# A decoder layer on one core: where the differences of a weight matrix are formed, and in which order two stages get their operands

## The chip, the cores and the metric

One core of a Trainium2 chip runs the kernel. The metric is the device time of one execution in microseconds, lower is better. The engines are TensorE (PE; its weight loads are PEld in the profile), VectorE (DVE), ScalarE (ACT), GpSimd (POOL) and SyncE (SP), whose queue issues all the transfers of this kernel, in order.

## The reference

One layer in float32 over 16 meta tokens and 1024 tokens of width 2048 (batch 1), followed by a final norm that drops the meta tokens:

```python
h = rmsnorm(x, gain)
q, k, v, g_attn, u, g_pool, m_attn, m_pool = split(h @ w_in)
o_attn = stick_breaking_attention(q, k, v) * silu(g_attn)     # 8 heads of 128
y_attn = o_attn @ w_attn_up                                   # (1024 -> 2048)
o_pool = (multiscale_pool(u) @ pool_w) * pool_scale * silu(g_pool)
y_pool = o_pool @ w_pool_up                                   # (1024 -> 2048)
merged = sigmoid(m_attn) * y_attn + sigmoid(m_pool) * y_pool
out = rmsnorm(x + merged @ w_out, final_gain)
```

## The kernel before, in words

Every matrix product is done in three matmuls: each operand is split into a high part (ACT copies it to a shorter float, L116) and a low part (the difference, L117, on DVE or POOL), and high times high, high times low and low times high are summed in one accumulator (`mm3`, L137 to L140; the last stage writes the three out in L1007 to L1009).

The large products, by `w_in` and by `w_out`, are cut in two by two blocks and done with seven block products instead of eight (Strassen's scheme in Winograd's form). This needs sums of blocks of both factors. For `w_out` these are four differences per block position: with b11, b12, b21, b22 its four blocks, T1 = b12 - b11 (form 2), b12 - b22 (form 1), b11 - (b12 - b22) (form 0) and b21 - (b11 - (b12 - b22)) (form 3). They don't depend on the tokens. `w_forms` (L183) forms them on POOL (L194), 256 columns at a time, from blocks loaded by SP (L190), and stores them to DRAM in `d_wf` (L195); the last stage loads them as weights. `w_forms` is a generator, and its steps are taken between the products of the attention stage: `between[0]` is called behind each of the three products of a pair of column blocks (`duo`). Form 2 is made from b12 and b11 loaded a second time, since the first copies are overwritten.

The stages in order of time: norm and transposes; the projections by `w_in`; the pooling branch; the attention stage (1174 to 1910 us), which for each of eight heads finishes the head's projections and lets the attention of the head (`attention`, L733) run step by step between matmuls of the next projections; the merges; the last stage.

In a step of attention, `scores` (L734) has PE form the scores, ACT two sigmoids (L743, L744), POOL mask the diagonal block (L748), DVE run a product scan (L753) and a product (L754), and two steps later `turn` (L763) has PE transpose the result (L769) for a split (L116, L117) and the product with the values.

The merges (1910 to 2275 us) do 32 products in the order of the list `order`: for a block of 128 output columns, `p` is the pooling branch (by `w_pu`) and `a` the attention branch (by `w_au`). Each has two halves of 512 tokens, 24 matmuls each, and two weight tiles that `load_w` loads and splits (`wr`, `wh`, `wl`, four buffers each). DVE multiplies each result by its gate (`sp`, `sa`, six buffers each, L965 and L970), POOL adds the two branches (L971), and for every second `a` product `sums` (L943) has POOL form four sums (L949) and SP store seven tensors to `d_f` (L957). The operands `op` and `oa` are filled ahead of the loop by `fill` (L908): a load to `ol` (six buffers) and a split.

The last stage multiplies by `w_out`: `prod` (L1000) loads a weight tile per step `j`, and `step` fills the next operand (`fill_f`, L1013, tiles `mr`, two buffers) and loads a row of `x`. Its first operand is A11, filled ahead of the first product (L1036) from `d_f[0]`.

The order of the instructions on each engine's queue is set by the framework's scheduler, by data, buffers and place in the program; `tc.keep_in_program_order` pins an instruction behind the one traced before it on its engine, and `tc.issue_after(ins)` puts what its block traces on the engine of `ins` behind `ins`. Tiles of a pool that is opened later take the memory of pools that were closed.

Of the kernel before, what the change touches and what calls it, by code (L numbers as in the profile page):

```python
# [9 lines left out]
F32 = mybir.dt.float32  # L10
# [5 lines left out]
P = 128  # L16
# [56 lines left out]
def trunk_kernel(  # L73
# [109 lines left out]
    def w_forms(pool):  # L183

        for p, j, i in ((p, j, i) for p in range(2) for j in range(KH) for i in range(2)):
            c = slice(i * 256, (i + 1) * 256)

            def block_of(tag, kh, nh):
                t = pool.tile([P, 256], F32, tag=tag, name=nm("cw"), bufs=1)
                tc.keep_in_program_order(nc.sync.dma_start(t, w_block(p, j, kh, nh)[:, c]))  # L190
                return t

            def minus(n, a, b):
                tc.keep_in_program_order(nc.gpsimd.tensor_tensor(out=a, in0=a, in1=b, op=ALU.subtract))  # L194
                tc.keep_in_program_order(nc.sync.dma_start(w_form(n)(p, j)[:, c], a))  # L195
                return a

            b12, b22 = block_of("cw0", 0, 1), block_of("cw1", 1, 1)
            b11, b21 = block_of("cw2", 0, 0), block_of("cw3", 1, 0)
            yield  # L200
            t2 = minus(0, b11, minus(1, b12, b22))
            minus(3, b21, t2)
            yield
            b12, b11 = block_of("cw1", 0, 1), block_of("cw0", 0, 0)
            yield
            minus(2, b12, b11)
# [22 lines left out]
    with ExitStack() as actx:  # L229
# [343 lines left out]
        def duo_steps(d, dst, post, dstm=None, step=None, again=False):  # L573
# [4 lines left out]
            def part(tag, src):  # L578
                t = ub.tile([P, HALF], F32, tag=tag, name=nm(tag), bufs=1)
                nc.sync.dma_start(t, src[d.n])  # L580
                return t
# [43 lines left out]
        between = [lambda: None]  # L625

        def duo(*args):
            for call in duo_steps(*args):
                call()
                between[0]()  # L630
# [10 lines left out]
        with ExitStack() as a0ctx:  # L641
# [24 lines left out]
            def silu_duo(*args):  # L666
                for call in silu_steps(*args):
                    call()
                    between[0]()
# [51 lines left out]
        with tc.tile_pool(name="a1", bufs=1, side="right", reuse_waits="tile") as a1:  # L721
# [127 lines left out]
            forms = w_forms(a1)  # L849
            between[0] = lambda: next(forms, None)  # L850
# [40 lines left out]
            for _ in forms:  # L891
                pass
# [13 lines left out]
    with tc.tile_pool(name="pm", bufs=2, side="right", reuse_waits="tile") as pm:  # L906

        def fill(A, j, src):  # L908
            raw = pm.tile([P, 512], F32, tag="ol", name=nm("ol"), bufs=6)
            nc.sync.dma_start(raw, src)  # L910
            put(A, j, raw)

        def fill_up(A, d_o, t):
            for j in range(KH):
                fill(A, j, d_o[j][:, t * HALF : (t + 1) * HALF])

        def up_mm(w, o, c):

            ops = [load_w(w_src(w, q, c * P)) for q in range(2)]
# [15 lines left out]
        for n, k in enumerate((("p", 0), ("p", KH), ("p", 1))):  # L935
            order.remove(k)
            order.insert(n, k)
        op, oa = [xquads(0, HALF, xo), xquads(1, HALF, xo)], [xquads(2, HALF), xquads(3, HALF, xc)]
        for t in range(2):
            fill_up(op[t], d_op, t)  # L940
        sps, ms = {}, {}

        def sums(j):  # L943
# [12 lines left out]
            for n, t in enumerate((a11, a12, r2, r3, r1, a22, r4)):  # L956
                nc.sync.dma_start(d_f[n][j], t)  # L957

        for n, (kind, c) in enumerate(order):
            if n in (0, 1):  # L960
                fill_up(oa[n], d_oa, n)
            if kind == "p":
                gs = [gate("sp", 6, d_sp, c, t) for t in range(2)]
                for t, a in up_mm(w_pu, op, c):
                    nc.vector.tensor_tensor(out=gs[t], in0=a, in1=gs[t], op=ALU.mult)  # L965
                sps[c] = gs
            else:
                gs = [gate("sa", 6, d_sa, c, t) for t in range(2)]
                for t, a in up_mm(w_au, oa, c):
                    nc.vector.tensor_tensor(out=gs[t], in0=a, in1=gs[t], op=ALU.mult)  # L970
                    nc.gpsimd.tensor_tensor(out=gs[t], in0=gs[t], in1=sps[c][t], op=ALU.add)  # L971
                ms[c] = gs
                if c >= KH:
                    sums(c - KH)

# [59 lines left out]
    A11, A12 = xquads(0, HALF, xo), xquads(1, HALF, xo)  # L1035
    for call in fills((A11, 0)):  # L1036
        call()
# [147 lines left out]
```

## Time and profile before

| | |
|---|---|
| median of three runs | 2612.1 us (2606.89 to 2615.9) |
| the profiled execution, its own time | 2615.75 us |
| its span, first to last instruction | 2614.0 us |
| mean granted clock of PE | 0.983 |
| PE busy | 2468.5 us, 94% of the span |
| POOL busy | 1034.6 us, 40% |
| DVE, ACT busy | 1253.8 us, 896.0 us |
| moved by DMA | 466 MB, 178 GB/s over the span |

Busy time is the time in which an engine executes; waits, register work and the issue of transfers don't count. The span leaves out 1.75 us of the execution's own time. PE is the busiest engine by far, and a wait of another engine matters only where PE waits for what that engine makes.

### The profile page before, as it was taken

The page shows a single profiled execution, that of the slowest core. Times are in us where ns is not written, and L with a number is a line of the kernel's source. Part 1 is how long each engine was busy: PE and PEld are TensorE (multiplying, and loading weights), DVE is VectorE, ACT ScalarE, POOL GpSimd, SP SyncE. Part 2 cuts the span into 40 slices and gives each one's busy share as a digit, 9 for nine tenths or more (in the row PEclk, how much of TensorE's full clock was granted, in tenths as well). Part 3 has the DMA queues.
Part 4 walks back from the last instruction along what each step waited for, and adds up shares of the span by engine and source line. Part 5 has one row for each costly group of instructions (what it writes and reads, how often), then busy time and mean ns, then how long its engine had stood idle before and what let it go on. Part 6 is the DMA issues. An engine that isn't in the chain of part 4 may idle for free. (4 is left out here: it accounts for less than half of the span.)

```text
span 2614.0 us, 36254 instructions
## 1 busy us (share of the span) xinstructions
PE 2468.5 (94%) x12680; PEld 2088.1 (80%) x12680; DVE 1253.8 (48%) x2089; ACT 896.0 (34%) x1845; POOL 1034.6 (40%) x962
## 2 busy tenths in 40 slices
PE   6898999999999999899999999999889999899998
PEld 5676778888888887887887888888768888677887
DVE  5432234543333344675575566557652222255456
ACT  6421122222222234224454454445441111044243
POOL 1665555554454534235445544554303222210212
PEclk8999999999999999999999999999989999999999
DMA  5566555665555557436556656554575444375544
GB/s 179 162 206 214 192 192 204 216 226 180 182 182 177 185 186 219 126 126 187 178 174 183 187 165 191 182 177 141 164 239 173 138 143 135 116 238 185 183 132 169
DMA packets 418168, 466.24 MB, mean 178 GB/s; under 512 B 35505, under 2 KB 278577, under 8 KB 416945
## 3 DMA queue, kind: packets, MB, share of 16 engines
q1 hardware_dynamic: 417984, 463.93, 55.8%
q8 instruction: 99, 1.62, 0.3%
q14 instruction: 85, 0.69, 0.1%
HBM read 321.50 MB, written 142.31 MB: 177 GB/s over the span
## 5 line engine op out<-in xcount | busy, mean ns | idle before, releaser
L138 PE MATMUL acc<-x,wh 128*128 128x512 f32 (+2 forms) x2736 | 980.2, 359 | 27.6 <-ACT wh L116 18.5
L140 PE MATMUL acc<-x,wl 128*128 128x512 f32 (+2 forms) x2736 | 971.1, 355 | 8.9 <-DVE wl L117 7.5
L139 PE MATMUL acc<-x,wh 128*128 128x512 f32 (+2 forms) x2736 | 968.8, 354 | 0.0
L138 PEld LDWEIGHTS acc<-x,wh 128*128 128x128 f32 x2736 | 520.1, 190 | 98.6 <-ACT wh L116 24.2
L140 PEld LDWEIGHTS acc<-x,wl 128*128 128x128 f32 x2736 | 518.6, 190 | 86.4 <-DVE wl L117 14.5
L139 PEld LDWEIGHTS acc<-x,wh 128*128 128x128 f32 x2736 | 519.3, 190 | 62.8
L116 ACT ACTIVATE wh<-wr 128x512 fp32r<-128x512 f32 x408 | 256.4, 630 | 580.6 <-PE accb L139 273.2
L117 DVE TENSOR_TENSOR wl<-wr,wh 128x512 fp32r<-128x512 f32 x288 | 217.2, 756 | 241.4 <-ACT wh L116 230.2
L117 DVE TENSOR_TENSOR wl<-r,wh 128x512 fp32r<-128x512 f32 x160 | 150.4, 944 | 339.3 <-ACT wh L116 315.2
L271 POOL TENSOR_TENSOR r<-raw,raw 128x512 f32<-128x512 f32 x80 | 111.7, 1396 | 378.8 <-DMA raw<-in_w_in_dram 357.0
L116 ACT ACTIVATE wh<-r 128x512 fp32r<-128x512 f32 x160 | 100.3, 632 | 469.7 <-POOL r L271 363.8
L117 POOL TENSOR_TENSOR wl<-wr,wh 128x512 fp32r<-128x512 f32 x120 | 171.8, 1431 | 224.0 <-ACT wh L116 170.6
L271 POOL TENSOR_TENSOR r<-r,raw 128x512 f32<-128x512 f32 x160 | 221.4, 1384 | 12.5 <-DMA raw<-in_w_in_dram 2.5
L138 PE MATMUL accb<-x,wh 128*128 128x512 f32 x512 | 200.5, 392 | 12.4 <-ACT x L116 12.4
L139 PE MATMUL accb<-x,wh 128*128 128x512 f32 x512 | 200.7, 392 | 0.0
L140 PE MATMUL accb<-x,wl 128*128 128x512 f32 x512 | 200.2, 391 | 0.0
L1007 PE MATMUL accb<-wh,x 128*128 128x512 f32 x416 | 163.8, 394 | 15.6 <-ACT x L116 13.3
L753 DVE TENSOR_TENSOR_SCAN wt<-wt 128x272 f32<-128x272 f32 (+5 forms) x128 | 109.8, 858 | 142.9 <-POOL wt L748 105.0
L194 POOL TENSOR_TENSOR cw<-cw,cw 128x256 f32<-128x256 f32 x128 | 106.1, 829 | 172.5 <-DMA cw<-in_w_out_dram 152.4
L1009 PE MATMUL accb<-wl,x 128*128 128x512 f32 x416 | 164.0, 394 | 2.5 <-DVE wl L117 2.3
L1008 PE MATMUL accb<-wh,x 128*128 128x512 f32 x416 | 163.3, 393 | 0.0
L971 POOL TENSOR_TENSOR sa<-sa,sp 128x512 f32<-128x512 f32 x32 | 47.2, 1475 | 275.4 <-DVE sa L970 265.9
(176 smaller groups left out, 3124.0 us busy)
## 6 DMA issues: line engine op xcount, KB each, us to landing
raw<-in_w_in_dram SPq DMA_DIRECT2D x96, 512.0 KB, 6.0
d_r<-r SPq DMA_DIRECT2D x160, 256.0 KB, 2.0
wr<-d_r SPq DMA_DIRECT2D x160, 256.0 KB, 3.3
raw<-in_w_in_dram SPq DMA_DIRECT2D x152, 256.0 KB, 5.3
cw<-in_w_out_dram SPq DMA_DIRECT2D x192, 128.0 KB, 3.2
wr<-in_w_in_dram SPq DMA_DIRECT2D x80, 256.0 KB, 3.0
d_wf<-cw SPq DMA_DIRECT2D x128, 128.0 KB, 2.0
wr<-d_wf SPq DMA_DIRECT2D x64, 256.0 KB, 2.8
```

Source lines behind the costliest of these rows:

```text
L116: nc.scalar.activation(hi, src, AF.Copy)
L117: (eng or nc.vector).tensor_tensor(out=lo, in0=src, in1=hi.bitcast(F32), op=ALU.subtract)
L138: nc.tensor.matmul(ps, wh, rh, start=first, stop=False, skip_group_check=skip)
L139: nc.tensor.matmul(ps, wh, rl, start=False, stop=False, skip_group_check=skip)
L140: nc.tensor.matmul(ps, wl, rh, start=False, stop=last, skip_group_check=skip)
L194: tc.keep_in_program_order(nc.gpsimd.tensor_tensor(out=a, in0=a, in1=b, op=ALU.subtract))
L271: nc.gpsimd.tensor_tensor(out=t, in0=a, in1=b, op=ALU.add)
L753: nc.vector.tensor_tensor_scan(out=rev, data0=rev, data1=rev, initial=wt[:, w : w + 1], op0=ALU.mult, op1=ALU.bypass)
L971: nc.gpsimd.tensor_tensor(out=gs[t], in0=gs[t], in1=sps[c][t], op=ALU.add)
L1007: nc.tensor.matmul(a, sh, wh, start=first and j == 0, stop=False, skip_group_check=not first)
L1008: nc.tensor.matmul(a, sl, wh, start=False, stop=False, skip_group_check=not first)
L1009: nc.tensor.matmul(a, sh, wl, start=False, stop=j == KH - 1, skip_group_check=not first)
```

## The change

The four forms are made during the merges, from tiles of 512 columns, so in 16 rounds instead of 32; each block is loaded once (form 2 gets a tile of its own, `cw4`). One or two steps of the generator are taken behind each of the 32 products: the loads of a round behind one product, its four subtracts and stores behind the next. In the attention stage the hook `between` goes. The tiles `up` and `nu` of a product pair get two buffers each (the pool's default).

At the start of the merges the two gate tiles of the first product are requested first, then the operands; the weights of the first product are issued behind the sixth operand load. In the merges the tensors 0, 1 and 5 of `d_f` are stored as soon as they are there, not with the sums. A11 is loaded and split in the merges, through their `ol` tiles, behind the last but one product.

```diff
     def w_forms(pool):
-        for p, j, i in ((p, j, i) for p in range(2) for j in range(KH) for i in range(2)):
-            c = slice(i * 256, (i + 1) * 256)
+        for p, j in ((p, j) for p in range(2) for j in range(KH)):
             def block_of(tag, kh, nh):
-                t = pool.tile([P, 256], F32, tag=tag, name=nm("cw"), bufs=1)
-                tc.keep_in_program_order(nc.sync.dma_start(t, w_block(p, j, kh, nh)[:, c]))
+                t = pool.tile([P, 512], F32, tag=tag, name=nm("cw"), bufs=1)
+                tc.keep_in_program_order(nc.sync.dma_start(t, w_block(p, j, kh, nh)))
                 return t
-            def minus(n, a, b):
-                tc.keep_in_program_order(nc.gpsimd.tensor_tensor(out=a, in0=a, in1=b, op=ALU.subtract))
-                tc.keep_in_program_order(nc.sync.dma_start(w_form(n)(p, j)[:, c], a))
-                return a
+            def minus(f, out, a, b):
+                tc.keep_in_program_order(nc.gpsimd.tensor_tensor(out=out, in0=a, in1=b, op=ALU.subtract))
+                tc.keep_in_program_order(nc.sync.dma_start(w_form(f)(p, j), out))
             b12, b22 = block_of("cw0", 0, 1), block_of("cw1", 1, 1)
             b11, b21 = block_of("cw2", 0, 0), block_of("cw3", 1, 0)
             yield
-            t2 = minus(0, b11, minus(1, b12, b22))
-            minus(3, b21, t2)
+            t1 = pool.tile([P, 512], F32, tag="cw4", name=nm("cw"), bufs=1)
+            minus(2, t1, b12, b11)
+            minus(1, b12, b12, b22)
             yield
-            b12, b11 = block_of("cw1", 0, 1), block_of("cw0", 0, 0)
+            minus(0, b11, b11, b12)
+            minus(3, b21, b21, b11)
             yield
-            minus(2, b12, b11)
...
-                t = ub.tile([P, HALF], F32, tag=tag, name=nm(tag), bufs=1)
+                t = ub.tile([P, HALF], F32, tag=tag, name=nm(tag))
                 nc.sync.dma_start(t, src[d.n])
...
-        between = [lambda: None]
         def duo(*args):
             for call in duo_steps(*args):
                 call()
-                between[0]()
...
-            forms = w_forms(a1)
-            between[0] = lambda: next(forms, None)
...
             gate_duo(gates.pop(0), None)
-            for _ in forms:
-                pass
...
         def fill(A, j, src):
             raw = pm.tile([P, 512], F32, tag="ol", name=nm("ol"), bufs=6)
-            nc.sync.dma_start(raw, src)
+            ins = nc.sync.dma_start(raw, src)
             put(A, j, raw)
+            return ins
         def fill_up(A, d_o, t):
-            for j in range(KH):
-                fill(A, j, d_o[j][:, t * HALF : (t + 1) * HALF])
-        def up_mm(w, o, c):
-            ops = [load_w(w_src(w, q, c * P)) for q in range(2)]
+            return [fill(A, j, d_o[j][:, t * HALF : (t + 1) * HALF]) for j in range(KH)][5]
+        def up_mm(w, o, c, behind):
+            with tc.issue_after(behind.ins) if behind is not None else nullcontext():
+                ops = [load_w(w_src(w, q, c * P)) for q in range(2)]
...
+        first = [gate("sp", 6, d_sp, 0, t) for t in range(2)]
         op, oa = [xquads(0, HALF, xo), xquads(1, HALF, xo)], [xquads(2, HALF), xquads(3, HALF, xc)]
-        for t in range(2):
-            fill_up(op[t], d_op, t)
+        behind = [fill_up(op[t], d_op, t) for t in range(2)][0]
...
-            for n, t in enumerate((a11, a12, r2, r3, r1, a22, r4)):
+            for n, t in ((2, r2), (3, r3), (4, r1), (6, r4)):
                 nc.sync.dma_start(d_f[n][j], t)
+        forms = w_forms(pm)
         for n, (kind, c) in enumerate(order):
...
             if kind == "p":
-                gs = [gate("sp", 6, d_sp, c, t) for t in range(2)]
-                for t, a in up_mm(w_pu, op, c):
+                gs = [gate("sp", 6, d_sp, c, t) for t in range(2)] if n else first
+                for t, a in up_mm(w_pu, op, c, None if n else behind):
...
                 ms[c] = gs
+                nc.sync.dma_start(d_f[c // KH][c % KH], gs[0])
                 if c >= KH:
+                    nc.sync.dma_start(d_f[5][c - KH], gs[1])
                     sums(c - KH)
+            for _ in range(2 if n % 2 else 1):
+                next(forms, None)
+            if (kind, c) == ("p", KC - 1):
+                for _ in forms:
+                    pass
+                A11 = xquads(0, HALF, xo)
+                for j in range(KH):
+                    fill(A11, j, d_f[0][j])
...
-    A11, A12 = xquads(0, HALF, xo), xquads(1, HALF, xo)
-    for call in fills((A11, 0)):
-        call()
+    A12 = xquads(1, HALF, xo)
     R2, R3 = xquads(2, HALF), xquads(3, HALF, xc)
```

## Rows read from the trace of the kernel before

**Rows 1.** The first part of the page: the busy time of each engine, its share of the span and its number of instructions.

```profile
PE 2468.5 (94%) x12680; PEld 2088.1 (80%) x12680; DVE 1253.8 (48%) x2089; ACT 896.0 (34%) x1845; POOL 1034.6 (40%) x962
```

**Rows 2.** The table of stretches, cut at the borders of the attention stage, the merges and the last stage. Columns: the stretch and its length; busy us and instructions of PE, PEld, DVE, ACT and POOL; the granted clock of PE; the share of DMA; GB/s.

```profile
1174.00:1910.00 736.00, 699.44 (x4091) 606.46 (x4090) 448.85 (x908) 354.01 (x838) 345.46 (x460) 1.00 0.57 176
1910.00:2275.00 365.00, 352.10 (x1537) 290.03 (x1536) 106.65 (x161) 60.71 (x98) 81.88 (x61) 0.98 0.49 156
2275.00:2614.00 339.00, 313.14 (x1440) 258.25 (x1440) 179.99 (x310) 129.43 (x257) 58.33 (x41) 0.97 0.56 182
```

**Rows 3.** The waits of PE, the first three rows in the attention stage, the fourth in the merges, the fifth in the last stage. Columns: us in total, times, the longest.

```profile
PE tr L769 <- DVE bt L754: 15.1, 8, 3.4
PE tr L769 <- DVE wt L751: 11.2, 9, 2.1
PE tr L769 <- DVE aT L117: 6.6, 12, 0.8
PE accb L138 <- ACT x L116: 12.4, 1, 12.4
PE accb L1007 <- ACT x L116: 13.3, 1, 13.3
```

**Rows 4.** From the listing of PE in order of time, in the attention stage: the first and the last wait on L754, one on L117 and one on L751. Columns: start, us, engine, line, operation, tile, count, and in brackets the idle time before and what ended it.

```profile
1213.11 0.33 PE L769 MATMUL tr<-ident,bt 128*128 128x128 f32 x1 [2.07 <-DVE bt L754]
1217.17 0.44 PE L769 MATMUL tr<-ident,bt 128*128 128x128 f32 x2 [0.62 <-DVE aT L117]
1241.06 0.55 PE L769 MATMUL tr<-ident,bt 128*128 128x128 f32 x3 [1.09 <-DVE wt L751]
...
1840.18 0.43 PE L769 MATMUL tr<-ident,bt 128*128 128x128 f32 x1 [3.40 <-DVE bt L754]
```

**Rows 5.** All engines in order of time around the last wait on L754, without the rows that don't bear on it.

```profile
1833.73 1.30 POOL L647 TENSOR_TENSOR gs<-zz,sg 128x512 f32<-128x512 f32 x1
1833.93 0.38 SPq L190 DMA_DIRECT2D cw<-in_w_out_dram  x1
...
1838.19 0.72 POOL L194 TENSOR_TENSOR cw<-cw,cw 128x256 f32<-128x256 f32 x1 [3.12 <-DMA cw<-in_w_out_dram]
1838.86 0.29 POOL L748 TENSOR_SCALAR_AFFINE_SELECT wt<-wt 128x128 f32<-128x128 f32 x1
...
1839.19 0.52 DVE L753 TENSOR_TENSOR_SCAN wt<-wt 128x144 f32<-128x144 f32 x1 [7.83 <-POOL wt L748]
```

**Rows 6.** In the attention stage: POOL's wait for the blocks of w_out, the group of its subtracts (us busy, mean ns), and from the listings in order of time a split on POOL with a product of DVE beside it, and a product of the same shape while POOL stood idle.

```profile
POOL cw L194 <- DMA cw<-in_w_out_dram: 145.3, 52, 8.0
L194 POOL TENSOR_TENSOR cw<-cw,cw 128x256 f32<-128x256 f32 x127 | 105.4, 830 | 165.5 <-DMA cw<-in_w_out_dram 145.3 <-issue 8.1 <-PE tr L769 7.0
...
1603.63 1.29 POOL L117 TENSOR_TENSOR wl<-wr,wh 128x512 fp32r<-128x512 f32 x1
1603.92 1.41 DVE L754 TENSOR_TENSOR bt<-bt,wt 128x384 f32<-128x384 f32 x1
...
1888.72 0.56 DVE L754 TENSOR_TENSOR bt<-bt,wt 128x384 f32<-128x384 f32 x1
```

**Rows 7.** Around the border of the attention stage and the merges, in order of time: the first weight load of the merges on SP, the last gate store, the last block loads of w_out, their subtract, the operand loads of the merges, and PE's first matmul.

```profile
1880.83 2.91 SPq L124 DMA_DIRECT2D wr<-in_w_pool_up_dram  x2
...
1911.94 0.43 SPq L844 DMA_DIRECT2D d_sp<-st  x1
1912.41 1.16 SPq L190 DMA_DIRECT2D cw<-in_w_out_dram  x2
...
1917.13 0.72 POOL L194 TENSOR_TENSOR cw<-cw,cw 128x256 f32<-128x256 f32 x1 [7.03 <-DMA cw<-in_w_out_dram]
1918.31 13.81 SPq L910 DMA_DIRECT2D ol<-d_op  x16
...
1922.49 0.80 PE L138 MATMUL accb<-x,wh 128*128 128x512 f32 x1 [12.40 <-ACT x L116]
```

**Rows 8.** The table of stretches (columns as in rows 2) behind each of the two gaps.

```profile
1922.50:1928.90 6.40, 6.40 (x14) 4.75 (x15) 4.77 (x8) 4.35 (x7) 0.00 (x0) 0.50 0.84 275
1929.30:1935.00 5.70, 5.70 (x26) 4.49 (x25) 4.35 (x8) 4.33 (x7) 0.00 (x0) 1.00 0.86 278
2287.80:2294.20 6.40, 6.40 (x14) 4.76 (x15) 3.01 (x5) 2.46 (x4) 0.00 (x0) 0.50 0.83 276
```

**Rows 9.** Around the border of the merges and the last stage, in order of time: POOL's last adds, the operand loads of the last stage, PE's first matmul, and the ninth weight load of the last stage.

```profile
2279.52 2.60 POOL L949 TENSOR_TENSOR r<-r,sa 128x512 f32<-128x512 f32 x2
...
2283.06 0.88 SPq L1015 DMA_DIRECT2D mr<-d_f  x2
...
2287.77 0.80 PE L1007 MATMUL accb<-wh,x 128*128 128x512 f32 x1 [13.26 <-ACT x L116]
...
2294.55 0.42 SPq L124 DMA_DIRECT2D wr<-in_w_out_dram  x1
```

**Rows 10.** In the merges: two groups of POOL's adds (us busy, mean ns, idle before), and SP's waits (us in total, times, the longest).

```profile
L971 POOL TENSOR_TENSOR sa<-sa,sp 128x512 f32<-128x512 f32 x31 | 45.6, 1470 | 271.2 <-DVE sa L970 261.8 <-DMA wr<-in_w_pool_up_dram 9.4
L949 POOL TENSOR_TENSOR r<-r,sa 128x512 f32<-128x512 f32 x14 | 18.1, 1293 | 0.5
...
SPq L957 <- POOL sa L971: 107.5, 22, 5.9
SPq L124 <- DVE wl L117: 86.3, 45, 7.6
```

More of the change, by code (lines that the diff above doesn't have):

```diff
@@ L1 @@
 import math
-from contextlib import ExitStack
+from contextlib import ExitStack, nullcontext
 import concourse.bass as bass
@@ L668, in silu_duo @@
                     call()
-                    between[0]()
             def sil_tiles():
@@ L968, in trunk_kernel @@
                 gs = [gate("sa", 6, d_sa, c, t) for t in range(2)]
-                for t, a in up_mm(w_au, oa, c):
+                for t, a in up_mm(w_au, oa, c, None):
                     nc.vector.tensor_tensor(out=gs[t], in0=a, in1=gs[t], op=ALU.mult)
```

## The prediction, made before the change was run

> **What bounds the kernel now.** I read the page first. In a span of 2614.0 us TensorE (PE) is busy for 2468.5 us, 94% [rows 1]: what can be won without fewer matmuls is the idle time of PE, at most 146 us, and whatever its clock loses. Next the table of stretches [rows 2], cut at the stage borders: the attention stage (1174 to 1910 us) has PE busy for 699.4 of 736 us, the merges (1910 to 2275) for 352.1 of 365, the last stage for 313.1 of 339. So idle time near the change is 36.6, 12.9 and 25.9 us. Then the waits of PE in each of these stretches [rows 3]. In attention they are many and short, nearly all on one line, the transposes L769: 15.1 us on the product L754, 11.2 us behind the copy L751, 6.6 us behind the split L117. In the merges there is one wait, 12.4 us, the first matmul on the split of its operand; in the last stage again one large one, 13.3 us, of the same kind. Around both gaps the table of stretches shows the granted clock [rows 8]: 0.50 for the 6.4 us behind each gap (the 1.2 GHz level), 1.00 before and after.
>
> Now what each wait ends on. Attention has eight heads, and the listing of PE shows for each head the same three waits: eight of 0.9 to 3.4 us on L754, seven of 0.6 us on L117, eight of 0.7 to 2.1 us mostly on L751 (the first and the last, or one, of each kind in [rows 4]). The instructions of all engines around the last of the first kind [rows 5] show its cause: GpSimd (POOL) ends the gating product L647 at 1835.0 us, then stands in front of a subtract of w_out (L194) whose block was issued only at 1833.9 us and lands 3.1 us of idle time later; behind it in POOL's queue waits the mask L748, and behind that the scan L753, the product L754 and the transpose. I looked at the other fifteen waits of the first and third kind in the same view: in each, L748 runs directly behind an L194 that had waited 2 to 5 us. The sums agree: L194 waited 145.3 us for its blocks in this stage and took 105.4 us itself [rows 6].
>
> At the first border [rows 7] the queue of SP decides. The last gate store is issued at 1911.9 us; then come two block loads of w_out, and the store of their difference, which waits for the subtract at 1917.1 us. Only at 1918.3 us does the first operand load of the merges go out, and PE starts 4.2 us later. At the second border [rows 9] the operand loads of the last stage go out at 2283.1 us, behind the stores of the last sums (POOL's last add starts at 2279.5 us), and PE starts at 2287.8 us.
>
> **The change, part by part.** *The block work leaves the attention stage.* Removed are 128 subtracts, 192 loads and 128 stores of 128 KB. All eight waits of the first kind end on a mask held up by L194. In [rows 4, 5] the mask could start at 1835.1 us in place of 1838.9, so the transpose, 1.3 us behind it, would be ready at about 1836.4, and PE came for it at 1836.8 (1840.18 less its wait of 3.40). I count the whole 15.1 us. For the eight of the third kind the scan behind them gets 0.65 to 2.1 us earlier; of 11.2 us in that row (which holds a few others) I count 8. The 6.6 us behind L117 I do not count. Against this I set 3 us for waits that appear when PE arrives earlier (the next in line are L751 and the split of the transposed block). Together 20 us; bounds: 10 (only half of the first kind and a third of the third goes) and 29 (all three rows but the last four microseconds).
>
> On this term a rule of the Trainium skill bears. [Rows 6] show the product L754 at 1.41 us for 384 columns while POOL ran a split beside it and at 0.56 us for the same shape while POOL was idle. The Trainium skill, GPSIMD Engine Reference, section 1. Specifications, has POOL and VectorE (DVE) share their SBUF interfaces, with contention for DVE instructions that have two SBUF inputs; the rows agree. By that rule 105 us less of POOL work would also shorten DVE's part and take some 4 us of the waits behind L117; the sum below would be 41 us instead of 37.
>
> *The up and nu tiles of each product pair get a second buffer.* No wait of PE ends on them; 0.
>
> *The first border.* Without block loads at the end, the next thing behind the last gate store (1911.9) is, by the new order, two gate loads and six operand loads, 0.43 us each, then the weights of the first product, pinned behind the sixth operand. In the old run nothing of a later pool was issued before the last store of the stage before, while weights, which need no new pool, ran ahead from 1880.8 us on [rows 7], so I take the operand loads to stay behind that store. First operand: issued at about 1912.8 instead of 1918.3, so 5.5 us earlier. But now weights of the first product come after it: ten loads of 256 KB at the 275 GB/s of [rows 8] last 9.5 us, so that product could start near 1922 us, as now. The second product's weights are not pinned; if PE takes that one first, the start is at 1917 us, and the operand splits, which now share their queue with two more weights, hold it for about 2 us. I take 3.5 us; bounds 0 and 15 (the whole gap of 12.4 us and 3 us of low clock, 14 matmuls at 0.43 instead of 0.23 us apart, if the loads run ahead of the last store after all).
>
> *The second border.* The operands of the last stage (A11) are loaded through buffers of the merges, at the last but one product; their data were stored long before (the last of them one product earlier), and the tiles they fill come free in the middle of that product, some 16 us before PE ends the merges (32 products in the 352 us of [rows 2] are 11 us each, and one and a half of them are left). Eight loads and eight splits (0.63 us on ScalarE, 0.69 on DVE) fit in 16 us. So the gap of 13.3 us goes, with the low clock behind it: 3 us. What is late next: weights of the last stage. The ninth is issued at 2294.6 us [rows 9], behind loads that wait for buffers; with PE starting at 2274.4 it is needed 21.8 us later, at 2296.2, and is ready at about 2299. With eight operand loads fewer in that queue it should be earlier; I set 2 us against the gain. 14.4 us; bounds 8 (weights late three times) and 16.4.
>
> *The block work enters the merges.* 64 subtracts of 512 columns (1.29 us each by the adds L949 of [rows 10], 83 us), 64 loads and 64 stores of 256 KB. POOL is busy for 81.9 of 365 us there [rows 2]; with 83 us more it is at 45%. DMA: 156 GB/s become about 255, below the 275 of [rows 8]. Loads are traced one product ahead of their subtracts, 11 us against the 3 to 5 us they take, so POOL should not stand and wait as it did. SP's stores wait for POOL: four stores in 5.2 us at the end of every second product, 13 us when two adds L971 and four of the sums come first. Behind them wait weights and gates. The weights have four buffers, two products (21.8 us) of lead; the wait of the weight loads in [rows 10] is for a free buffer, not for data. Cost: 1 us; bounds 0 and 12.
>
> Sum: 20 + 3.5 + 14.4 - 1 = 37 us. The profiled execution took 2615.75 us, which gives 2578.8; the median of the runs before is 2612.1, 3.65 us lower, and from it the sum gives 2575. I forecast 2576 us.
>
> **Rivals.** (a) *The attention waits stay*: another load or the next instruction of DVE takes L194's place. For it: seven waits of 0.6 us end on DVE as it is. Against: in [rows 5] POOL has nothing else to do for 3.1 us. Gain 17 us, 2595 us. (b) *The second gap stays*: A11's loads keep their place in SP's queue behind the last sums' stores. For it: stores of the blocks are pinned there too. Against: their buffers are free. Gain 23 us, 2589 us. (c) *Both gaps close and attention loses all its waits*: 15 + 16.4 + 29 less 1, so 59 us, 2553 us; it needs operand loads ahead of the last gate store, against which [rows 7] speak. (d) *The merges starve*: SP stands in front of a block store while weights wait behind it, and PE, which has no cover there but the two products' lead, stops in each product. It decides from 1.2 us per product on (32 products, 37 us); at 2 us each the time would be 2639 us. For it: POOL work in that stage doubles and every store of it is pinned in SP's order. Against: no wait of PE in the merges now, and 107 us of SP's waits on POOL already pass unnoticed there.
>
> **How the numbers follow.** Forecast (2562 to 2590) 0.60; (a) 0.15; (b) 0.08; (c) 0.10; (d) 0.07. The range for 8 in 10 takes in the forecast's bounds, (b), (a) and part of (c): 2560 to 2597 us. A measurement of this kernel tells about 0.3%, 8 us, from no change. Faster by more than that: all but (d) and the edge of (a), 0.92; within it 0.04; slower 0.04, from (d).
>
> **What will show it.** Right: PE's waits on L769 fall from 33 us to below 15; the first matmul of the merges waits 6 to 12 us; the first one of the last stage waits under 2 us, at clock 1.00; no wait of PE between the borders. Wrong: waits on weight splits (wh, wl) in the merges or early in the last stage, a granted clock of 0.50 inside the merges, or POOL waiting for cw loads there.

## The result, and the profile after

The changed kernel takes 2591.6 us, median of 6 runs (2586.9 to 2597.7), beside 2613.3 for the kernel before on the same chips: a ratio of 0.9918, 95% interval 0.9897 to 0.9938, or 22 us less. Forecast were 2576 us in a range of 2560 to 2597. The range holds the time, but the sum behind it does not fit term by term: one term was too small by 10 us and one had the wrong sign. That the time lies in the range is in part luck: had attention given only the 20 us counted for it, and all else come as it did, the time would have been about 2602 us.

The profiled execution took 2589.8 us, its span 2588.1. First the same reading as [rows 1, 2], of the changed kernel: busy time of TensorE (PE) and POOL by the page, then the stretches, here cut exactly at PE's own borders: attention from its first transposes to its last product, the first gap, the merges, the last stage, and the low clock inside the last stage.

```profile
PE 2462.5 (95%) x12680; PEld 2087.6 (81%) x12680; DVE 1268.1 (49%) x2089; ACT 896.8 (35%) x1845; POOL 1005.4 (39%) x898
```

```profile
1182.10:1876.40 694.30, 683.82 (x3994) 596.13 (x3992) 443.71 (x893) 346.86 (x827) 227.17 (x329) 1.00 0.39 120
1876.40:1907.60 31.20, 0.07 (x2) 0.04 (x1) 16.69 (x26) 16.20 (x26) 0.00 (x0) 0.57 0.85 267
1907.60:2259.40 351.80, 350.48 (x1537) 289.62 (x1538) 111.42 (x146) 51.26 (x83) 167.49 (x123) 0.99 0.73 239
2259.40:2588.10 328.70, 313.09 (x1441) 256.91 (x1439) 176.29 (x302) 126.55 (x250) 59.63 (x43) 0.98 0.56 184
2292.70:2298.20 5.50, 5.50 (x14) 3.83 (x14) 2.94 (x5) 1.90 (x3) 0.00 (x0) 0.59 0.63 226
```

The attention stage of the kernel before, cut in the same way:

```profile
1185.80:1910.10 724.30, 687.73 (x3994) 594.66 (x3992) 443.19 (x896) 350.45 (x831) 337.88 (x453) 1.00 0.57 175
```

So attention is 30.0 us shorter. The gap in front of the merges grew from 12.4 us [rows 7] to 31.2. The gap in front of the last stage, 13.3 us [rows 9], is gone: PE ends the merges and goes on at once, at a clock of 1.00. The last stage itself became 2.5 us longer. From the start of attention on this is 1428.2 us before and 1406.0 after, 22.2 less; the stages ahead of attention, which the change does not touch, differ by 3.7 us between the two executions.

PE's waits after the change, to be held against [rows 3] (L764 was L769, L746 was L751, L1010 was L1007): columns are us in total, times, the longest.

```profile
PE accb L138 <- ACT wh L116: 32.4, 2, 31.1
PE accb L1010 <- ACT wh L116: 7.0, 3, 5.6
PE tr L764 <- DVE wt L746: 7.0, 9, 1.6
PE tr L764 <- DVE aT L117: 1.0, 2, 0.6
```

The waits on the product in attention (15.1 us) have no row left. Both large rows now end on `wh`, the split of a weight, where [rows 3] ended on `x`, an operand. SP's queue shows why, for the first of them, in order of time (start, us, engine, line, operation):

```profile
1872.42 5.75 SPq L839 DMA_DIRECT2D d_sp<-st  x2
1878.26 0.88 SPq L923 DMA_DIRECT2D sp<-d_sp  x2
1879.23 14.19 SPq L901 DMA_DIRECT2D ol<-d_op  x16
1894.01 6.69 SPq L901 DMA_DIRECT2D ol<-d_oa  x8
1900.75 0.97 SPq L124 DMA_DIRECT2D wr<-in_w_pool_up_dram  x2
...
1906.88 0.63 ACT L116 ACTIVATE wh<-wr 128x512 fp32r<-128x512 f32 x1 [0.21 <-DMA wr<-in_w_pool_up_dram]
...
1907.56 0.80 PE L138 MATMUL accb<-x,wh 128*128 128x512 f32 x1 [31.13 <-ACT wh L116]
```

The operand loads go out right behind the last gate store and two gate loads, as forecast. But the two weights of the first product, in [rows 7] on their way 31 us ahead of the last gate store, now stand behind 24 operand loads and go out 22.5 us behind that store.

### The profile page after: what moved, and what is told of

It reads as the page before. It is cut to its first block, busy times and chain, and to the rows that moved or that the text cites. A ratio compares the mean times of both kernels' runs of the same rounds, so it can differ in the third digit from the quotient of the medians.

```text
span 2588.1 us, 35874 instructions
## 1 busy us (share of the span) xinstructions
PE 2462.5 (95%) x12680; PEld 2087.6 (81%) x12680; DVE 1268.1 (49%) x2089; ACT 896.8 (35%) x1845; POOL 1005.4 (39%) x898
## 4 chain that ended last, share of the span: by engine, by line
PE 77%; DMA 7%; DVE 6%; POOL 3%; ACT 2%; issue 2%; SPq 0%; DVEq 0%; POOLq 0%; ACTq 0%
PE acc L138 17%; PE acc L140 17%; PE acc L139 17%; PE accb L138 4%; PE accb L139 4%; PE accb L140 4%; POOL r L270 3%; PE accb L1012 2%; PE accb L1011 2%; PE accb L1010 2%; DMA mr<-d_f 2%; DMA raw<-in_w_in_dram 2%; PE tr L764 1%; DVE s L692 1%; DVE x L117 1%
## 5 line engine op out<-in xcount | busy, mean ns | idle before, releaser
L140 PEld LDWEIGHTS acc<-x,wl 128*128 128x128 f32 x2736 | 518.3, 189 | 85.3 <-DVE wl L117 13.3
L117 DVE TENSOR_TENSOR wl<-wr,wh 128x512 fp32r<-128x512 f32 x288 | 221.1, 770 | 248.2 <-ACT wh L116 230.0
L117 DVE TENSOR_TENSOR wl<-r,wh 128x512 fp32r<-128x512 f32 x160 | 149.5, 938 | 345.6 <-ACT wh L116 328.5
L117 POOL TENSOR_TENSOR wl<-wr,wh 128x512 fp32r<-128x512 f32 x120 | 166.6, 1388 | 346.0 <-ACT wh L116 289.3
L1010 PE MATMUL accb<-wh,x 128*128 128x512 f32 x416 | 163.8, 394 | 7.1 <-ACT wh L116 7.0
L117 DVE TENSOR_TENSOR wl<-raw,wh 128x512 fp32r<-128x512 f32 x136 | 102.6, 765 | 100.9 <-ACT wh L116 100.8
L116 ACT ACTIVATE wh<-raw 128x512 fp32r<-128x512 f32 x160 | 97.6, 624 | 135.2 <-PE acc L139 100.3
```

Source lines behind the costliest of these rows:

```text
L116: nc.scalar.activation(hi, src, AF.Copy)
L117: (eng or nc.vector).tensor_tensor(out=lo, in0=src, in1=hi.bitcast(F32), op=ALU.subtract)
L140: nc.tensor.matmul(ps, wl, rh, start=False, stop=last, skip_group_check=skip)
L1010: nc.tensor.matmul(a, sh, wh, start=first and j == 0, stop=False, skip_group_check=not first)
```

## The experiments

The stages of each kernel are in one table, each row from one profiled execution: PE's own borders in us, and the sum from the start of attention on. The last column is the ratio of the median time to that of the kernel before on the same chips, with its 95% interval. The kernels ran on different chips, so a difference of two medians is given beside the difference of the sums where the two part.

| kernel | attention | first gap | merges | second gap | last stage | sum | ratio |
|---|---|---|---|---|---|---|---|
| before | 724.3 | 12.4 | 352.0 | 13.3 | 326.2 | 1428.2 | 1 |
| changed | 694.3 | 31.2 | 351.8 | 0 | 328.7 | 1406.0 | 0.9918 (0.9897 to 0.9938) |
| no_pin | 694.3 | 10.3 | 352.2 | 0 | 325.9 | 1382.7 | 0.9832 (0.9816 to 0.9848) |
| blocks_only | 694.3 | 8.8 | 356.8 | 13.2 | 326.6 | 1399.7 | 0.9896 (0.9879 to 0.9912) |
| borders_only | 725.8 | 34.2 | 350.0 | 0 | 325.8 | 1435.8 | 1.0042 (1.0022 to 1.0063) |
| late_a11 | 694.3 | 29.4 | 357.3 | 13.2 | 325.7 | 1419.9 | 0.9961 (0.9947 to 0.9975) |
| no_blocks | 694.3 | 31.1 | 350.1 | 0 | 325.5 | 1401.0 | 0.9876 (0.9860 to 0.9891) |
| no_pin_rows | 694.3 | 9.6 | 352.3 | 0 | 324.5 | 1380.7 | 0.9798 (0.9776 to 0.9820) |
| no_pin_spread | 694.4 | 10.5 | 352.5 | 0 | 323.2 | 1380.6 | 0.9792 (0.9771 to 0.9814) |

**The pin alone (no_pin).**

```
-                for t, a in up_mm(w_pu, op, c, None if n else behind):
+                for t, a in up_mm(w_pu, op, c, None):
```

> The changed kernel with one edit: the weights of the first product of the merges are no longer pinned behind the sixth operand load. Theory A (SP's order makes the first gap): with the pin the two weight loads stand behind 24 operand loads in SP's queue (issued at 1900.75 us, 22.5 us behind the last gate store), without it they run ahead of the last gate store as in the kernel before; PE then waits for the first operand alone, about 8 us in place of 31.1, and the operands behind it, 0.89 us apart, keep just ahead of it; about 21 us less than the changed kernel, 2570 us. Theory B (the operand loads set the start whatever the order): weights that run ahead only shift the operand loads, PE starts early and stops at every operand, and the first product ends where it ends now; less than 8 us gained, 2584 us or more.

Measured: 2569.0 us, 23 us less than the changed kernel; the interval of its ratio (0.9816 to 0.9848) lies clear of that of the changed kernel. SP's queue and PE's first matmul of the merges:

```profile
1867.62 0.37 SPq L124 DMA_DIRECT2D wr<-in_w_pool_up_dram  x1
...
1879.94 3.20 SPq L124 DMA_DIRECT2D wr<-in_w_attn_up_dram  x2
1883.23 0.46 SPq L839 DMA_DIRECT2D d_sp<-st  x1
1883.74 0.96 SPq L923 DMA_DIRECT2D sp<-d_sp  x2
...
1891.67 0.79 PE L138 MATMUL accb<-x,wh 128*128 128x512 f32 x1 [10.26 <-ACT x L116]
```

Eight weight loads, those of four products, again run ahead of the last gate store (1883.23 us; the rows show three of the eight), and the wait ends on an operand. PE does not stop at every operand behind it: the merges last 352.2 us, as before. Theory A holds. Of the 31.2 us, 20.9 were the place of the weights in the queue; the other 10.3 are the wait for the first operand, which goes out behind the last gate store.

**The block work alone (blocks_only).** The kernel before, with `w_forms` in its new form and these edits to the two stages:

```
...
-            forms = w_forms(a1)
-            between[0] = lambda: next(forms, None)
...
+        forms = w_forms(pm)
...
+            for _ in range(2 if n % 2 else 1):
+                next(forms, None)
...
```

> The kernel before with one part of the change alone: the block work of w_out leaves the attention stage and stands in the merges, in its new form; the gate loads, the pin, the sums' stores and the loads of the last stage stay as before. Theory A (the gain in attention comes from the block work alone): the waits of PE on the transposes fall from 33 us to about 8 as in the changed kernel and attention ends some 33 us earlier; the weights of the first product, not pinned, run ahead, so the first gap is 8 to 9 us in place of 12.4; the second gap stays at 13 us with 3 us of low clock: about 36 us less than before, 2577 us, so faster than the changed kernel by some 15 us. Theory B (the block work starves the merges unless the rest of the change stands beside it, or the second buffers of up and nu have a share in attention): waits of PE between the borders or transposes still waiting over 15 us, 2595 us or more.

Measured: 2584.1 us, 29 us less than before, and attention at 694.3 us, although up and nu have one buffer here: their second buffer is worth nothing. The first gap is 8.8 us, as theory A said. The merges are 5 us longer than before, by one late weight 50 us into them (3.5 us) and the low clock behind it; on that point theory B is right in kind. By the traces this one part of the change gives more than the whole change, 28.5 us in place of 22.2; the intervals of the two ratios overlap.

**The rest of the change alone (borders_only).** The changed kernel with the block work put back into attention, in its old form, and with one buffer each for `up` and `nu`:

```
...
+            forms = w_forms(a1)
+            between[0] = lambda: next(forms, None)
...
-        forms = w_forms(pm)
...
```

> The changed kernel with one part undone: the block work stands in the attention stage as in the kernel before (up and nu with one buffer again); the gates ahead of the operands, the pin, the sums' stores and the early loads of A11 stay. Theory A (the parts add up): attention takes 724.3 us as before; at the first border the last block loads and their store still hold the operand loads back as they did (12.4 us), and the pin puts the weights behind 24 operand loads, 21 us more; at the second border 10.6 us are won as in the changed kernel. 12 us more than before, 2624 us. Theory B (the block work in attention and the pin hide behind one another: while SP waits for the last blocks the weights would not have been late): the first gap stays near 15 us, 2605 us, a little less than before.

Measured: 2624.5 us, 10 us more than before. The first gap is 34.2 us, and it ends on a weight again:

```profile
1914.12 0.33 SPq L195 DMA_DIRECT2D d_wf<-cw  x1
1914.54 0.88 SPq L932 DMA_DIRECT2D sp<-d_sp  x2
1915.47 14.77 SPq L910 DMA_DIRECT2D ol<-d_op  x16
1930.57 6.23 SPq L910 DMA_DIRECT2D ol<-d_oa  x8
1936.85 0.99 SPq L124 DMA_DIRECT2D wr<-in_w_pool_up_dram  x2
```

Theory A holds: the last store of the blocks holds the operand loads until 1915.5 us, 7 us behind PE's end (1908.3), and then the weights come as late behind them as in the changed kernel. The parts add up: -28.5 us (blocks_only) and +7.6 us give -20.9, against -22.2 for the whole.

**What in the block work cost attention 30 us.** Three kernels made from the one before, read in the attention stage alone, one execution of each. All three leave out the differences of `w_out`, so what they return is not the layer's result. The first keeps subtracts and stores, and loads blocks once; each subtract takes the fourth block from itself (att_noload):

```
...
-            b12, b22 = block_of("cw0", 0, 1), block_of("cw1", 1, 1)
-            b11, b21 = block_of("cw2", 0, 0), block_of("cw3", 1, 0)
...
+            if b is None:
+                b = block_of("cw0", 0, 1), block_of("cw1", 1, 1), block_of("cw2", 0, 0), block_of("cw3", 1, 0)
...
```

> The kernel before with all subtracts and stores of the block work left in the attention stage, but only four block loads in all, at its start (each later subtract takes the fourth of these blocks from itself, so the differences of w_out are left out). POOL's work stays, its wait for blocks goes. The attention stage, from its first transposes to its last product, takes 724.3 us before and 694.3 us with the block work moved away. Theory A (the waits come from a subtract that stands and waits for its block): nearly the whole gain is there, 694 to 698 us, with no wait on L754 left. Theory B (POOL's 105 us of subtracts, by standing ahead of the masks or by slowing DVE, make up a good part of the 30 us): 704 to 715 us, with waits on L754 and behind the splits L117 still there.

The second keeps loads and stores without a subtract (att_nosub):

```
-                tc.keep_in_program_order(nc.gpsimd.tensor_tensor(out=a, in0=a, in1=b, op=ALU.subtract))
```

> The kernel before with all block loads and stores left in the attention stage and no subtract (the loaded block itself is stored, so the differences of w_out are left out). Nothing of the block work is left on POOL; the DMA traffic and SP's queue stay as they are. Theory A (POOL's queue is the cause, for whichever reason): the attention stage takes 694 to 697 us in place of 724.3. Theory C (the traffic of 176 GB/s, or SP standing in front of block stores, makes weights and other loads late): 705 us or more, with POOL free of waits for blocks.

Measured: 700.1 us, between the two theories, and 694.7 us, as theory A said. So the traffic and SP's queue cost 0.4 us, and it is POOL. But the first run did not take all waiting away: its subtracts waited for the store of the tile they write.

```profile
POOL cw L195 <- DMA d_wf<-cw: 72.3, 24, 5.1
```

So the third keeps the subtracts alone: two blocks are loaded once, every subtract takes one from the other, and nothing is stored (att_subonly):

```
...
-                tc.keep_in_program_order(nc.sync.dma_start(w_form(n)(p, j)[:, c], a))
...
```

> The kernel before with the 128 subtracts of the block work alone left in the attention stage: two blocks are loaded once, nothing is stored, and every subtract takes one of them from the other (the differences of w_out are left out, the last stage takes a block of w_out itself in their place). No subtract waits for a load or for a store. The attention stage takes 724.3 us before, 694.3 with the block work moved away, 700.1 with subtracts and stores alone, where POOL still stood 72 us in front of tiles whose store had not landed. Theory A (waiting is all of it): 694 to 696 us. Theory B (POOL's time in subtracts, standing ahead of the masks, makes the rest): 698 to 701 us, with the waits behind the copy and the splits as in the run with the stores.

Measured: 703.4 us. PE's waits in attention, and POOL's subtracts:

```profile
PE tr L764 <- DVE wt L746: 12.8, 9, 1.6
PE tr L764 <- DVE aT L117: 1.9, 4, 0.7
...
L189 POOL TENSOR_TENSOR cw<-cw,cw 128x256 f32<-128x256 f32 x125 | 103.0, 837 | 0.6
```

No subtract waits (0.6 us idle ahead of 125 of them), no wait on the product is left, and still 9.1 of the 30.0 us remain, more than the 4 to 7 of theory B. So it is theory B in kind: 20.9 us went with the loads, the stores and the waits for them, and as loads and stores without a subtract cost 0.4 us, these were subtracts that stood waiting; 9.1 us are left with POOL's 103 us of work itself. The split is not sharp: the first run, where POOL waited 72.3 us for stores, was 3.3 us shorter than this one, so something beside waiting and working time counts, perhaps when a subtract runs. No run shows what. Of the 9.1 us, 5.8 stand in the row on L746 (12.8 us, 7.0 in the changed kernel). Whether POOL's work costs by standing ahead of the masks or by slowing DVE (below) the runs do not separate.

**A11 as before (late_a11).**

```
-                A11 = xquads(0, HALF, xo)
-                for j in range(KH):
-                    fill(A11, j, d_f[0][j])
...
+    for call in fills((A11, 0)):
+        call()
...
```

> The changed kernel with one part undone: the operands A11 of the last stage are loaded as before, behind the stores of the last sums. Theory A (the early loads take the whole second gap away, and a late weight gives back part): PE waits about 13 us for the first operand of the last stage, with 3 us of low clock behind it, and the wait of 5.6 us on a weight at 2292 us with its 2.3 us of low clock goes; about 9 us more than the changed kernel, 2600 us. Theory B (the second gap only moved into the late weight): within 3 us of the changed kernel, 2589 to 2595 us.

Measured: 2603.7 us, 12 us more than the changed kernel (13.9 by the sums). The second gap is back at 13.2 us and the last stage is 3.0 us shorter. Theory A holds. The merges are also 5.5 us longer: the second product waits 3.1 us for its weight, where it waits 1.3 us in the changed kernel, and behind that wait PE runs for 6.6 us at a clock of 0.54, where the changed kernel keeps 1.00 behind its shorter one (first the wait, then the stretch behind it):

```profile
1927.43 0.79 PE L138 MATMUL accb<-x,wh 128*128 128x512 f32 x1 [3.05 <-ACT wh L116]
1927.40:1934.00 6.60, 6.57 (x17) 5.20 (x18) 1.89 (x3) 1.64 (x3) 0.00 (x0) 0.54 1.07 362
```

That is 1.7 us of wait and 3.7 us of PE's busy time. The first gap is 1.8 us shorter here, so PE comes sooner for a weight that goes out as late behind that of the first product (16.0 us, 15.3 in the changed kernel). Why the first weights land sooner the edit does not explain, and it stays open.

**No block work at all (no_blocks).**

```
-        return lambda p, j: d_wf[n][p][:, j * 512 : (j + 1) * 512]
+        return lambda p, j: w_block(p, j, 0, 0)
...
-        forms = w_forms(pm)
+        forms = iter(())
```

The differences are left out, and the last stage loads a block of `w_out` in the place of each.

> The changed kernel without any block work: no loads, subtracts or stores of blocks of w_out, and the last stage takes a block of w_out itself wherever it took a difference (so that part of the computation is left out; the products and weight loads of the last stage stay as many). Theory A (in the merges the block work costs nothing, and the late weight of the last stage comes from SP's order there): the first gap 31 us less 2 for the four block loads between, the late weight as it is; within 4 us of the changed kernel, 2587 to 2592 us. Theory B (its traffic, 242 GB/s where there were 156, makes operands and weights late): the wait of 5.6 us with its 2.3 us of low clock goes, and 2 to 4 us more, 2580 us or less.

Measured: 2580.1 us. By the traces 5 us are won, 1.7 in the merges and 3.2 in the last stage; by the medians 12. Neither theory gives this: the median is about theory B's, but the wait on the late weight of the last stage, which theory B takes away, is still there without any block traffic:

```profile
2288.03 0.50 PE L1010 MATMUL accb<-wh,x 128*128 128x512 f32 x1 [4.60 <-ACT wh L116]
```

So the block work is not its cause; that it is the order of the queue (theory A) is tried next. But the block work is not free: 5 us by the traces, 12 by the medians.

**The late weight of the last stage (no_pin_rows, no_pin_spread).** In the changed kernel SP's queue runs so, at the start of the last stage:

```profile
2268.85 1.35 SPq L124 DMA_DIRECT2D wr<-in_w_out_dram  x3
2270.24 0.43 SPq L1018 DMA_DIRECT2D mr<-d_f  x1
...
2286.31 0.33 SPq L1018 DMA_DIRECT2D mr<-d_f  x1
2286.68 0.43 SPq L984 DMA_DIRECT2D row<-in_x_dram  x1
2287.15 0.43 SPq L124 DMA_DIRECT2D wr<-in_w_out_dram  x1
...
2292.68 0.79 PE L1010 MATMUL accb<-wh,x 128*128 128x512 f32 x1 [5.63 <-ACT wh L116]
```

Ten weights have gone out by 2270.2 us; the eleventh (the expectations call it the ninth, its number in the kernel before) stands behind seven operand loads, which go out as one of two buffers comes free, and the ten row loads between them. SP's largest wait from the start of the last stage to 2300 us is that of the operand loads for the split that frees a buffer:

```profile
SPq L1018 <- DVE x L117: 11.5, 8, 2.4
```

Two edits, each to the kernel without the pin: row loads eight steps later, and operands and rows both spread over twice the steps.

```
-[lambda b=b, c=c: load_row(0, b, c) for c in range(4) for b in range(HB)]
+[lambda: None] * 8 + [lambda b=b, c=c: load_row(0, b, c) for c in range(4) for b in range(HB)]
```

> The changed kernel without the pin, and in the last stage the sixteen loads of rows of x (256 KB each) begin eight steps later. Theory A (the ninth weight is late because in SP's queue it stands behind eight operand loads and eight row loads, which at 0.95 us each last 15 us): with the eight row loads out of the way it goes out some 7 us earlier, the wait of 5.1 us and its low clock go: 7 us less than without the pin alone, 2562 us. Theory B (the pace of the queue there is that of the operand loads alone, which wait for their two buffers, 2.2 us each): the ninth weight goes out within 2 us of where it did, and nothing is gained, 2567 to 2571 us.

```
...
+    a12 = [call for f in fills((A12, 1)) for call in (f, lambda: None)]
...
+    late = [call for r in row_calls[:8] for call in (lambda: None, r)] + [call for r in row_calls[8:] for call in (r, lambda: None)]
+    step = stepper(a12 + fills((R2, 2), (R3, 3)), late)
```

> The changed kernel without the pin, and in the last stage both the operand loads of A12 and the row loads are spread over twice as many steps (one operand and one row to two weights, in place of one of each to every weight). Theory A and theory B of the run with the later rows alike: the ninth weight stands behind four operand and four row loads and goes out 8 us earlier, PE's wait of 5.1 us and its low clock go, 2562 us; theory D (the DMA engines are full at 270 to 280 GB/s there and what is put off comes back as a late weight or operand further on): waits of PE on wh, wl or x later in the last stage, 2566 us or more.

Measured: 2567.0 and 2564.5 us, beside 2569.0 for the kernel without the pin; by the traces the last stage is 1.4 and 2.7 us shorter. In the first of them the eleventh weight goes out 12.7 us into the stage instead of 27.5:

```profile
2245.51 1.36 SPq L124 DMA_DIRECT2D wr<-in_w_out_dram  x3
2246.91 0.90 SPq L1018 DMA_DIRECT2D mr<-d_f  x2
2247.86 1.02 SPq L984 DMA_DIRECT2D row<-in_x_dram  x2
2248.99 0.38 SPq L124 DMA_DIRECT2D wr<-in_w_out_dram  x1
```

Theory A is right on the order and wrong on its worth. PE's wait of 5.1 us goes, and in its place come shorter ones in later steps; these are the rows of the last stage, no_pin_rows first, no_pin_spread in the second fence:

```profile
PE accb L1010 <- ACT wh L116: 2.6, 2, 1.8
PE accb L1012 <- DVE wl L117: 1.8, 3, 1.2
```

```profile
PE accb L1010 <- ACT wh L116: 2.7, 3, 2.0
PE accb L1012 <- DVE wl L117: 0.5, 2, 0.3
```

What is put off comes back as a later wait, as theory D has it; that full DMA engines are the reason is not shown, for in the first 40.7 us of the last stage of no_pin_rows their share was 0.79. The version with the spread loads has the shortest time here: 2564.5 us, 27 us less than the changed kernel by the medians and 25.4 by the sums, with a ratio of 0.9792 to the kernel before. Its lead over the kernel without the pin (2.1 us by the traces) is less than these runs can tell.

## Why the prediction was right and wrong, step by step

*Attention, 20 us counted: 30.0 measured, above the upper bound of 29.* The mechanism was right: the masks stood behind subtracts that waited, and the 15.1 us of the first kind went whole. The third kind gave 4.2 us (11.2 to 7.0) where 8 were counted. Mis-sized was what I left out: 5.6 us behind L117, counted at nothing (4.7 of them go with the waiting alone, in att_subonly); 1.3 us of another wait of the stage; and 3.9 us by which PE's own busy time is shorter (687.7 to 683.8), for a reason that the runs do not show. The 3 us of new waits did not come. The bounds took only the block's arrival for a cost; some 9 of the 30 us came with POOL's working time, as the run with the subtracts alone shows. The lower bound was also summed wrong: half of 15.1 and a third of 11.2 are 11.3, or 8.3 less the 3 us of new waits, and not 10.

*The 4 us for DVE beside POOL.* In attention DVE was busy for 443.2 us beside 337.9 us of POOL before, and for 443.7 beside 227.2 after. The equal sums hide two shifts. These are groups of DVE's instructions before (line, us busy, mean ns):

```profile
L754 DVE TENSOR_TENSOR bt<-bt,wt 128x272 f32<-128x272 f32 x40 | 30.4, 760 | 4.1
L117 DVE TENSOR_TENSOR wl<-wr,wh 128x512 fp32r<-128x512 f32 x94 | 69.3, 737 | 55.1 <-ACT wh L116 54.6
L754 DVE TENSOR_TENSOR bt<-bt,wt 128x400 f32<-128x400 f32 x16 | 10.7, 671 | 1.6
```

in the changed kernel:

```profile
L749 DVE TENSOR_TENSOR bt<-bt,wt 128x272 f32<-128x272 f32 x40 | 25.5, 638 | 4.1
L117 DVE TENSOR_TENSOR wl<-wr,wh 128x512 fp32r<-128x512 f32 x91 | 63.0, 692 | 47.8 <-ACT wh L116 46.7
L749 DVE TENSOR_TENSOR bt<-bt,wt 128x400 f32<-128x400 f32 x16 | 16.0, 1002 | 1.6
```

and with the subtracts alone, where DVE was busy for 458.8 us:

```profile
L749 DVE TENSOR_TENSOR bt<-bt,wt 128x272 f32<-128x272 f32 x40 | 33.1, 827 | 4.1
L117 DVE TENSOR_TENSOR wl<-wr,wh 128x512 fp32r<-128x512 f32 x94 | 71.2, 758 | 51.3 <-ACT wh L116 50.8
```

The product of 272 columns and the splits of the weights are longer in the two of these kernels that have the subtracts. But without them the product of 400 columns became longer, and so did a copy (385 to 470 ns, 64 times), which takes as much back; what these stand beside is shown for one product of 400 columns only, 1.41 us beside a split on POOL (1237.3 us, changed kernel), where another took 0.58 us with POOL idle. The Trainium skill, GPSIMD Engine Reference, section 1. Specifications, has POOL and DVE share their SBUF interfaces, with contention for DVE instructions that have two SBUF inputs. The two groups that the subtracts lengthen have two such inputs and agree with it. The 4 us were still no safe term: from before to after what DVE gained in some groups it lost in others, and 4.7 of the 5.6 us behind L117 went with the subtracts still there.

*First border, 3.5 us gained: 18.8 lost, far outside its bounds of 0 and 15.* This is the step that failed. I read "pinned behind the sixth operand load" as the place of the weights in the queue and counted ten loads. A pin only says what they may not pass. Once they cannot run ahead they stand where the code issues them, behind all sixteen loads of `op` and eight of `oa`. The same step hoped that PE would take the second product first; its weights went out later still (1916.0 us). The rest of the step was sound: without the pin the gap is 10.3 us, within the 6 to 12 given for the first matmul. And the row that should have warned me was quoted: weights on their way at 1880.8 us, 31 us ahead of the store [rows 7]. What ran ahead unasked was the cover of that border, and the pin took it away. No rival named this; all of them kept the first gap at 12.4 us or less. By the prediction's own signs it was wrong here: the first matmul of the merges waited 31.1 us in place of 6 to 12, and the waits are on a weight's split (`wh`), in the merges and early in the last stage.

*Second border, 14.4 us: 10.8.* The gap of 13.3 us went, as worked out (by its own terms, 13.3 and 3 less 2, the forecast is 14.3). "What is late next" was named rightly, weights of the last stage, but set at 2 us; it is 7.0 us of waits and 5.5 us at a clock of 0.59, so that the last stage is 2.5 us longer than before although the low clock behind the gap is gone.

*Block work in the merges, 1 us lost: 0.2 gained.* The merges did not starve (rival d): two waits of PE in all, the first gap and one of 1.3 us. POOL did wait for blocks, 50.5 us in three waits, 42.7 of them ahead of the first block. The prediction named that as a sign of being wrong; no wait of PE in the merges ends on POOL. Held against the kernel without block work it costs 1.7 us here and 3.2 in the last stage, within the bounds of 0 and 12; the 3.2 are in the term above.

*Second buffers of up and nu, 0:* shown by the run with the block work alone.

So the sum of 37 us came to 22 by errors of +10.0 us (attention), -22.3 (first border), -3.6 (second border) and +1.2 (merges). The range had been drawn wide for rivals that did not come about, (a) and (b), and it held the time because the error in attention made good nearly half of that at the first border.

## What to carry to other kernels

Before a load is pinned, look in the trace for how early it is issued now: a load that runs ahead of a stage border is cover, and one pin can cost more than the work moved away gives. A pin is a lower bound, so count what the code issues between the pin and the pinned load. And when work leaves an engine's queue, price both its waiting and its working time for what stands behind it.

## What the runs showed that was not expected

The stages ahead of attention have the same code in all these kernels, and from the start of the span to attention's first transposes they took between 1177.8 us (att_noload) and 1187.1 us (no_pin). The attention stage repeated to 0.1 us over seven kernels. A difference of some us between two spans says nothing of a change until it is placed in a stage.

The 275 GB/s that the forecast took for the pace of loads [rows 8] is not a ceiling. This is the stretch behind the first gap of the changed kernel, at 373 GB/s for 4.4 us:

```profile
1907.60:1912.00 4.40, 4.40 (x11) 3.44 (x12) 1.44 (x3) 1.41 (x3) 2.17 (x2) 0.55 1.03 373
```
